# Transposes by way of DRAM in a hybrid RWKV-7 / HGRN-2 layer on one core: blocks of turned tiles stored and loaded a row at a time, and fourteen head ends turned on VectorE instead of TensorE

## The chip, the core and the metric

The kernel runs on one NeuronCore of a Trainium2 chip, as one launch. Its engines run side by side, each through its own list of instructions in order: TensorE (PE, matmuls into PSUM), VectorE (DVE), ScalarE (ACT), GpSimd (POOL) and SyncE (SP), which issues nearly all DMAs. An instruction that waits holds up whatever stands behind it on its engine. The metric is the device time of one execution in microseconds (us); lower is better.

## The reference, cut to what matters

One layer over 512 frames of 2048 channels. A combined input projection feeds 16 RWKV heads of 64 channels and 8 HGRN heads of 128; their gated outputs go through one output projection, a residual and a LayerNorm. With the scans left to their names:

```python
proj = einsum('btd,dc->btc', h, w_in)
rw = token_shift(proj[..., :RWKV_COLS], shift_mu)
hg = proj[..., RWKV_COLS:]
# RWKV, per head of 64
o = rwkv7_scan(r, decay, k, v, -kk, kk * a)
o = (o - mean(o)) * rsqrt(var(o) + GN_EPS) * gn_w + gn_b
o = o + sum(r * k * r_k) * v
o_rwkv = o * silu(z)
# HGRN, per head of 128, in chunks of 64 frames
o = hgrn2_chunkwise(q, log_f, k, i)
o_hgrn = o * rsqrt(mean(o * o) + RMS_EPS) * g_norm_w * silu(z)
y = concat([o_rwkv, o_hgrn]) @ w_out
h = layer_norm(ALPHA * h + y, ln_w, ln_b)
```

All of it is float32; setup_inputs draws x, the weights and the gains.

## The kernel before, in words

**Stages.** Activations lie with channels on the 128 partitions and 512 frames along the free dimension. The input projection is a sequence of units; a unit is one block of 128 output channels, 16 steps over the input channels, and each step takes three products of 128x128 by 128x512 (`three`, L453 before; high and low parts of both operands, so that the sum has float32 accuracy). These go to PSUM banks with the tag `main`, and are called projection products below. Weights stream from `w_all` in pieces `wr` of 512 KB, two pieces buffered; ACT makes the high part `wh` of each half and DVE the low part `wl` (three buffers each). The output projection comes last: four column blocks of 512, the first of them (`d = 0`) over 16 gated channel blocks in the order 0 to 5, 8 to 13, 14, 6, 15, 7. These sixteen steps of the first block are called steps 0 to 15; step 11 takes block 13, step 12 block 14, step 13 block 6 and step 15 block 7. A gated block k is a tile `g`, split into `xh` (ACT) and `xl` (DVE) just before its step. Twelve of the gated blocks are put into the DRAM tensor `spill` and loaded back; 6, 7, 14 and 15 stay on chip. During step 8 the 2 MB of LayerNorm weights are loaded, broadcast to all partitions (`big<-ln_wb`).

**Mixers.** Beside the projections, and put in between their products, run the mixers. RWKV goes by pairs of heads (8 pairs, p = 0 to 7), two pairs to a group: `rwkv_prep`, then `rwkv_invert` and `rwkv_scan` for the group, then `outputs`, then `rwkv_finish` for each pair (group norm, bonus, gate). HGRN goes by head (h = 0 to 7), two at a time, ending in `hgrn_out`.

**What sets the order.** The order on each engine is written out when the program is built, by a planner (`Plan`): generators yield operations, and the planner puts an operation into its engine's list when, by its own cost table, the operands will be there. For a DMA the planner books a fixed time. Nothing is reordered on the chip.

**Turning.** Several tiles have to be transposed, from frames on the partitions to channels on the partitions or back:
- In `rwkv_prep`, `bk` (128 x 8 x 128) and `v` (128 x 512, into the lower half of `zz`) go through `turned`: one DVE transpose (`dtr`, L366), which turns each 32x32 block within itself, and then small DMAs, one for each 32x32-block position, that carry the blocks to their places from SBUF to SBUF (L401): 16 DMAs of 32 KB for each `bk`, 8 of 32 KB for each `v`.
- In `rwkv_finish` the normed output `o_all` is turned on TensorE: four transposes (`tr`, L328) into a PSUM bank `mix`, which DVE then reads in `stt`.
- In `hgrn_out` the same is done with four transposes of `o2`. Three further transposes for each head turn `k` earlier in that function.

Of the kernel before, what the change touches and what calls it, by code (L numbers as in the profile page):

```python
# [15 lines left out]
P = 128  # L16
# [225 lines left out]
def mixer_kernel(ctx, tc, head, x_r, w_all, par, up, ln_wb, consts, hmask, out):  # L242
# [148 lines left out]

    def turned(dst, src, tmp, rows=4, base=0):


        name = dst.tensor.name
        yield dtr(tmp, src)
        yield lambda: by_now(tmp)
        for a in range(4):
            for b in range(rows):
                o = base + 32 * b  # L400
                nc.sync.dma_start(dst[o : o + 32, :, 32 * a : 32 * a + 32],  # L401
                                  tmp[32 * a : 32 * a + 32, :, 32 * b : 32 * b + 32])
# [218 lines left out]

    hc = [slice(64 * h, 64 * h + 64) for h in range(2)]

    def rwkv_prep(S, p):
# [114 lines left out]
        yield room(zz=1)  # L739
        z = take("zz", [P, NCH, P])  # L740
        yield room(ksq=1)
        tmp = take("ksq")
        yield from turned(z, chunks(v), chunks(tmp), rows=2, base=64)
        drop(v, tmp)
        S["zz"] = z

    def from_v(SS, sc):

        yield lambda: all("zz" in S for S in SS)
        zs = [S["zz"] for S in SS]  # L750
        yield room(main=2, mix=1)
        yield landed(*zs, sc)
        pss = [take("main") for _ in SS]
        for half, (z, ps) in enumerate(zip(zs, pss)):
            for c in range(NCH):
                for h in range(2):
                    yield mm(ps[hc[h], c * C : c * C + C], sc[64:128, 0, half * 16 + 2 * c + h],
                             z[64:128, c, hc[h]])

        def keep():  # L760
            for z, ps in zip(zs, pss):
                for h in range(2):
                    yield copy(z[0:64, :, hc[h]], chunks(ps[hc[h]]))
                drop(ps)

        return keep

    def outputs(SS, sc):
# [3 lines left out]
        for half, (S, po) in enumerate(zip(SS, pss)):  # L772
            z = S["zz"]
            yield lambda z=z: by_now(z)
            for c in range(0, NCH, 2):
                for h in range(2):
                    for e in range(2):
                        yield mm(po[hc[e], c // 2 * P + 64 * h : c // 2 * P + 64 * h + 64],
                                 sc[:, 1, half * 16 + 2 * (c + e) + h], z[:, c + e, hc[h]])
        for S, po in zip(SS, pss):  # L780
# [51 lines left out]
    def rwkv_scan(SS, sc):  # L832
# [9 lines left out]
        def block(ps, h):  # L842
            return ps[hc[h], h * 64 : h * 64 + 64]

        for rt, bds, o in zip(rts, bdss, os):
            yield memset(rt[64:128], 0.0)
# [4 lines left out]
        for c in range(NCH):  # L851
            more = c < NCH - 1
            zs = [zz[:, c] for zz in zzs]
            news = [bds[c % 2] for bds in bdss]
            pxs = []
            if c > 0:
# [5 lines left out]
                for rt, px, z in zip(rts, pxs, zs):  # L862
                    yield stt(rt[0:64], px[0:64, :P], -1.0, z[0:64], ALU.mult, ALU.subtract)
                if more:
                    for new, old, pc in zip(news, olds, pcs):
                        yield act(new, old, AF.Copy, scale=pc[:, c : c + 1])
            else:
                for rt, z in zip(rts, zs):
                    yield copy(rt[0:64], z[0:64], scale=-1.0)
            yield landed(*rts)  # L870
# [5 lines left out]
            for psa, z in zip(psas, zs):  # L876
                for h in range(2):
                    yield copy(z[0:64, hc[h]], block(psa, h))
                drop(psa)
# [17 lines left out]
    def rwkv_finish(S, p):  # L897
# [31 lines left out]

    def rwkv_group(SS, grp):  # L930
# [4 lines left out]
        def run():  # L935
# [3 lines left out]
            for i, S in enumerate(SS):  # L939
                plan.add(finishes, rwkv_finish(S, 2 * grp + i))  # L940

# [115 lines left out]
    def hgrn_out(S, h, q, k, dt_, dg, tot, tots):  # L1057
# [37 lines left out]
        S["used"]()  # L1095
        yield landed(o2)
        pn = take("mix")
        for j in range(4):
            yield tr(pn[:, j * P : j * P + P], o2[:, j * P : j * P + P])
        yield has(S, "g")  # L1100
        yield stt(g, pn, hcol(HHW, h), S["g"], ALU.mult, ALU.mult)
        drop(S["g"], pn, o2)
        put_gated(8 + h, g)
# [28 lines left out]
    scans = [plan.queue(), plan.queue()]  # L1132
    groups, finishes, preps = plan.queue(), plan.queue(), plan.queue()
    heads, stores = plan.queue(), plan.queue()
# [532 lines left out]
```

## Time and profile before

| what | value |
|---|---|
| runs | median 1050.85 us of 3 (1050.78 to 1051.72) |
| the profiled execution's own time | 1050.24 us |
| its span, first to last instruction | 1048.5 us |
| granted TensorE clock | 0.999 |
| DMA packets, MB | 87305, 114.79 |
| packets under 512 bytes | 56368 |
| transposes on TensorE (L328) | 88 |
| DMAs at L401 | 192 of 32 KB |

Busy shares are averages over stages with different limits. In the lists of groups, the number behind the bar is the group's busy time and its mean duration in ns; durations of matmuls overlap, since their ends are modelled, so the distance between the starts of two matmuls is what one costs. "Idle before" is the time the engine stood before those instructions and what ended it.

### The profile page before, as it was taken

The page shows a single profiled execution, that of the slowest core. Times are in us where ns is not written, and L with a number is a line of the kernel's source. Part 1 is how long each engine was busy: PE and PEld are TensorE (multiplying, and loading weights), DVE is VectorE, ACT ScalarE, POOL GpSimd, SP SyncE. Part 2 cuts the span into 40 slices and gives each one's busy share as a digit, 9 for nine tenths or more (in the row PEclk, how much of TensorE's full clock was granted, in tenths as well). Part 3 has the DMA queues.
Part 4 walks back from the last instruction along what each step waited for, and adds up shares of the span by engine and source line. Part 5 has one row for each costly group of instructions (what it writes and reads, how often), then busy time and mean ns, then how long its engine had stood idle before and what let it go on. Part 6 is the DMA issues. An engine that isn't in the chain of part 4 may idle for free.

```text
span 1048.5 us, 18840 instructions
## 1 busy us (share of the span) xinstructions
PE 1040.6 (99%) x7342; PEld 865.1 (83%) x7342; DVE 755.7 (72%) x1653; ACT 437.6 (42%) x867; POOL 38.3 (4%) x81
## 2 busy tenths in 40 slices
PE   9999999999999999999999999999999999999997
PEld 8888888888888888888888888888888888888885
DVE  7465898667759987676689866865998778625556
ACT  6545333445353354452533353525334554323321
POOL 0000000000000000000000000000000002000000
PEclk9999999999999999999999999999999999999999
DMA  8134342222343522223534323234352244545613
GB/s 332 54 103 114 99 109 86 86 79 81 84 123 100 122 82 74 78 98 79 138 78 118 98 62 96 70 96 110 100 128 72 69 164 131 182 131 159 202 60 131
DMA packets 87305, 114.79 MB, mean 109 GB/s; under 512 B 56368, under 2 KB 58160, under 8 KB 87088
## 3 DMA queue, kind: packets, MB, share of 16 engines
q1 hardware_dynamic: 87072, 113.39, 36.6%
q8 instruction: 58, 0.95, 0.4%
q14 instruction: 31, 0.25, 0.1%
q10 hardware_dynamic: 144, 0.20, 0.1%
HBM read 99.92 MB, written 7.34 MB: 102 GB/s over the span
## 4 chain that ended last, share of the span: by engine, by line
PE 99%; DVE 1%; DVEq 0%; issue 0%
PE main L453 74%; PE mix L324 11%; PE mix L453 8%; PE main L1192 3%; PE main L324 2%; PE mix L328 1%; PE mix L1142 0%; DVE inv L356 0%; DVE inv L347 0%; DVE stats L1549 0%; DVEq L1663 0%; DVE mv L1357 0%; DVE bd L356 0%; DVE mv L352 0%; DVE inv L1140 0%
## 5 line engine op out<-in xcount | busy, mean ns | idle before, releaser
L453 PE MATMUL main<-xl,wh 128*128 128x512 f32 x864 | 341.1, 395 | 0.0
L453 PE MATMUL main<-xh,wl 128*128 128x512 f32 x864 | 341.1, 395 | 0.0
L453 PE MATMUL main<-xh,wh 128*128 128x512 f32 x864 | 340.9, 395 | 0.0
L337 ACT ACTIVATE wh<-wr 128x512 fp32r<-128x512 f32 x299 | 186.9, 627 | 237.1 <-PE main L453 180.5
L347 DVE TENSOR_TENSOR wl<-wr,wh 128x512 fp32r<-128x512 f32 x299 | 203.8, 682 | 61.8 <-ACT wh L337 60.1
L453 PEld LDWEIGHTS main<-xh,wh 128*128 128x128 f32 x864 | 162.4, 188 | 33.0
L453 PEld LDWEIGHTS main<-xh,wl 128*128 128x128 f32 x864 | 162.5, 188 | 32.6
L453 PEld LDWEIGHTS main<-xl,wh 128*128 128x128 f32 x864 | 162.4, 188 | 32.6
L453 PE MATMUL main<-wl,xh 128*128 128x512 f32 (+1 forms) x262 | 102.6, 392 | 0.0
L453 PE MATMUL main<-wh,xh 128*128 128x512 f32 (+1 forms) x262 | 102.1, 390 | 0.0
L453 PE MATMUL main<-wh,xl 128*128 128x512 f32 (+1 forms) x262 | 101.6, 388 | 0.0
L453 PEld LDWEIGHTS main<-wh,xh 128*128 128x128 f32 x262 | 49.2, 188 | 9.9
L453 PEld LDWEIGHTS main<-wh,xl 128*128 128x128 f32 x262 | 49.2, 188 | 9.7
L453 PEld LDWEIGHTS main<-wl,xh 128*128 128x128 f32 x262 | 49.2, 188 | 9.6
L338 ACT ACTIVATE t<-main,om 128x512 f32<-128x512 f32 x33 | 22.4, 687 | 51.1 <-PE main L453 41.6
L356 DVE SCALAR_TENSOR_TENSOR t<-main,pr,t 128x511 f32<-128x511 f32 x33 | 24.4, 747 | 26.5 <-ACT t L338 26.2
L347 DVE TENSOR_TENSOR inv<-inv,inv 64x30 f32<-64x30 f32 (+14 forms) x120 | 38.6, 322 | 2.9
L347 DVE TENSOR_TENSOR inv<-inv 64x30 f32<-64x30 f32 (+14 forms) x120 | 38.4, 320 | 2.3
L347 DVE TENSOR_TENSOR t<-t,tot 128x256 f32<-128x256 f32 x96 | 37.8, 414 | 1.8 <-PE mix L324 1.7
L356 DVE SCALAR_TENSOR_TENSOR bd<-mix,pc,bd 64x64 f32<-64x64 f32 x112 | 31.7, 283 | 7.5 <-PE mix L324 5.2
L337 ACT ACTIVATE zz<-mix 64x64 f32<-64x64 f32 x63 | 13.8, 220 | 46.9 <-PE mix L324 45.8
L338 ACT ACTIVATE t<-main 128x512 f32<-128x512 f32 x32 | 18.5, 598 | 30.7 <-PE main L453 30.2
(222 smaller groups left out, 1328.0 us busy)
## 6 DMA issues: line engine op xcount, KB each, us to landing
wr<-w_all SPq DMA_DIRECT2D x156, 512.0 KB, 3.6
q<-head SPq DMA_DIRECT2D x15, 448.0 KB, 5.9
q<-q SPq DMA_DIRECT2D x128, 32.0 KB, 2.4
g<-x_r SPq DMA_DIRECT2D x16, 256.0 KB, 3.8
spill<-g SPq DMA_DIRECT2D x12, 256.0 KB, 2.7
out<-q SPq DMA_DIRECT2D x12, 256.0 KB, 2.4
t<-spill SPq DMA_DIRECT2D x10, 256.0 KB, 4.2
zz<-ksq SPq DMA_DIRECT2D x64, 32.0 KB, 2.6
```

Of the source, the lines that this page charges most:

```text
L324: return Op([("pe", cost, lambda: pe.matmul(o, l, r, start=start, stop=stop, **kw))], [l, r], [o], mode="narrow" if narrow else "main" if ...
L328: return Op([("pe", 0.11, lambda: pe.transpose(o, i, ident))], [i], [o])
L337: return "act", cost, lambda: sc_e.activation(o, i, f, scale=scale)
L338: return "act", cost, lambda: sc_e.activation(o, i, f, scale=scale, bias=bias)
L347: return dve_op([a, b], o, lambda: dve.tensor_tensor(o, a, b, f), base=0.16 if o.shape[0] < P and size(o) == C and o.tensor.name in tags e ...
L356: return dve_op([a, b], o, lambda: dve.scalar_tensor_tensor(o, a, s, b, f1, f2), per=0.00113, base=0.085 if o.shape[0] == P else 0.25 if s ...
L453: pe.matmul(ps, l, r, start=first and i == 0, stop=last and i == 2)
L1192: pe.matmul(pss[a], *ops, start=k == 0 and low == of == 0, stop=k == KT - 1 and low == 1)
```

## The change

`turned` no longer places blocks from SBUF to SBUF. After the DVE transpose, whose result is now laid out by rows of blocks, one DMA stores the whole tile to a new DRAM tile `far` (512 KB for `bk`, 256 KB for the others), the generator waits until the planner's clock is 3.0 us on, and then one DMA for each row of blocks loads it into place: 4 loads of 128 KB for `bk`, 2 of 128 KB for `v`, 4 of 64 KB for the others. The planner books the data as there 4.5 us after the loads.

The result of `turned` for `bk` lands in the old `bk` tile in another layout, so a copy of 128 x 1024 brings it into `tmp`, which becomes `bk`. `zz` keeps the layout by blocks, and the code that reads it is changed to match.

The ends are turned in the same way: all eight `rwkv_finish`, and `hgrn_out` for heads 0 to 5 (heads 6 and 7 keep their TensorE transposes). In place of DVE's `stt` from PSUM, an ACT operation now applies the gain (and for RWKV the bias) while it reorders the blocks, and DVE multiplies from SBUF. The two pairs of a group now finish on two queues of the planner instead of one.

In all, the program has 5641 matmul instructions instead of 5697 (56 transposes fewer), 50 DVE transposes instead of 36, 863 ACT operations instead of 846, and 376 DMAs on SP instead of 434. Counted over the order, PE goes from projection products into products on part of the array (small tiles) 33 times instead of 30.

```diff
+    def turned(dst, src, tmp, base=0):
+        c = src.shape[1]
+        n = src.shape[2] // 32
+        yield dtr(tmp, src.rearrange("p c (b f) -> p b c f", f=32))
         yield lambda: by_now(tmp)
-        for a in range(4):
-            for b in range(rows):
-                o = base + 32 * b
-                nc.sync.dma_start(dst[o : o + 32, :, 32 * a : 32 * a + 32],
-                                  tmp[32 * a : 32 * a + 32, :, 32 * b : 32 * b + 32])
-            at = plan.clock["pe"] + 0.4 * rows
-            yield lambda: plan.clock["pe"] >= at
-        plan.ready[name] = (plan.clock["pe"] + 3.0, "dma")
+        far = dpool.tile([4, 32, n, c * 32], F32, tag=nm("far"), name=nm("far"))
+        nc.sync.dma_start(far.rearrange("a p b r -> (a p) b r"), tmp.rearrange("p b c f -> p b (c f)"))
+        plan.busy[tmp.tensor.name] = (plan.clock["pe"] + 3.0, "dma")
+        at = plan.clock["pe"] + 3.0
+        yield lambda: plan.clock["pe"] >= at
+        for b in range(n):
+            o = base + 32 * b
+            nc.sync.dma_start(dst[o : o + 32].rearrange("p a c f -> p a (c f)"),
+                              far[:, :, b].rearrange("a p r -> p a r"))
+        plan.ready[dst.tensor.name] = plan.busy[dst.tensor.name] = (plan.clock["pe"] + 4.5, "dma")
...
@@ rwkv_prep
-        yield from turned(bk, bk, tmp)
-        drop(tmp)
+        flat = bk.rearrange("p c t -> p (c t)")
+        yield from turned(blocks(flat, NCH), bk, blocks(tmp.rearrange("p c t -> p (c t)"), NCH))
+        yield copy(tmp.rearrange("p c (a f) -> p a c f", f=32), blocks(flat, NCH))
+        drop(bk)
+        S["bk"] = tmp
...
@@ rwkv_finish
-        drop(sm, sq)
+        drop(sm)
+        yield from turned(blocks(S["ot"], 4), o_all, blocks(sq.rearrange("p a b -> p (a b)"), 4))
+        drop(sq)
...
         sz = take("ksq")
...
-        yield landed(o_all)
-        po = take("mix")
-        for j in range(4):
-            yield tr(po[:, j * P : j * P + P], o_all[:, j])
         yield act(sz, z, AF.Tanh, scale=0.5)
-        yield stt(g, po, hcol(HGW, p), S["bv"], ALU.mult, ALU.add)
-        drop(po)
+        yield act(in_blocks(g), blocks(S["ot"], 4).rearrange("p a c f -> p c a f"), AF.Identity,
+                  scale=hcol(HGW, p), bias=hcol(HGB, p))
         yield stt(z, sz, 1.0, z, ALU.add, ALU.mult)
-        yield stt(g, g, hcol(HGB, p), z, ALU.add, ALU.mult)
+        yield tt(g, g, S["bv"], ALU.add)
+        yield tt(g, g, z)
...
@@ hgrn_out
+        if h < 6:
+            yield room(ksq=1)
+            tmp = take("ksq")
+            yield from turned(blocks(o2, 4), tiles(o2), blocks(tmp, 4))
+            drop(tmp)
+            yield has(S, "g")
+            yield act(in_blocks(g), blocks(o2, 4).rearrange("p a c f -> p c a f"), AF.Copy, scale=hcol(HHW, h))
+            yield tt(g, g, S["g"])
+            drop(S["g"], o2)
```

How the order moves is shown at three places, all in the first block of the output projection, where the last pairs (6 and 7) and the last HGRN head (7) finish.

TensorE, step 11 of that block, before: `main_8896` and `main_8938` are PSUM banks of the output, `xh_9338` and `xl_9339` the parts of gated block 13, `t_7607` the normed output of RWKV pair 7.

```order
L453 MATMUL main_8896<-wh_9318,xh_9338 128x512
L328 MATMUL mix_9368<-cst,t_7607 128x128 x4
L453 MATMUL main_8896<-wl_9319,xh_9338 128x512
L453 MATMUL main_8896<-wh_9318,xl_9339 128x512
L453 MATMUL main_8938<-wh_9318,xh_9338 128x512
```

The same step in the changed program; `xh_9270` is gated block 13 there, and `t_7899` the normed output of HGRN head 7.

```order
L464 MATMUL main_8861<-wh_9248,xh_9270 128x512
L464 MATMUL main_8861<-wl_9249,xh_9270 128x512
L328 MATMUL mix_9301<-cst,t_7899 128x128 x4
L464 MATMUL main_8861<-wh_9248,xl_9271 128x512
L464 MATMUL main_8869<-wh_9248,xh_9270 128x512
```

The transposes of pairs 6 and 7 are gone from PE's list; those of head 7 are the only ones left in the output projection, and stand at step 11.

ScalarE around the same step, before, with the counters that each instruction waits for: `xh_9338` is the split of block 13 (step 11), `ksq_9349` the tanh of pair 7's gate, `xh_9361` and `xh_9394` the splits for steps 12 and 13.

```order
L337 ACTIVATE xh_9307<-t_9179 128x512 [waits DMAHW4_49]
L337 ACTIVATE wh_9318<-wr_9199 128x512 [waits PE_49,Activation_49]
L337 ACTIVATE xh_9338<-t_9209 128x512 [waits DMAHW6_49]
L337 ACTIVATE wh_9351<-wr_9273 128x512 [waits DMAHW7_49,PE_49,Activation_49]
L337 ACTIVATE xh_9361<-g_9000 128x512
L338 ACTIVATE ksq_9349<-t_8898 128x512
L337 ACTIVATE wh_9382<-wr_9273 128x512 [waits DVE_49,PE_49]
L337 ACTIVATE xh_9394<-g_9227 128x512
```

And now, from the split for step 10 (`xh_9238`) on: `ksq_9265` is the tanh of pair 6's gate, `g_9264` the new operation that applies pair 6's gain to the loaded blocks.

```order
L337 ACTIVATE xh_9238<-t_9130 128x512 [waits DMAHW0_49]
L337 ACTIVATE wh_9248<-wr_9152 128x512 [waits PE_49,Activation_49]
L338 ACTIVATE ksq_9265<-t_8751 128x512 [waits DMAHW5_49,DVE_49]
L337 ACTIVATE xh_9270<-t_9158 128x512 [waits DMAHW2_49]
L337 ACTIVATE wh_9281<-wr_9202 128x512 [waits DMAHW3_49,PE_49,Activation_49]
L337 ACTIVATE xh_9293<-g_8890 128x512
L338 ACTIVATE g_9264<-t_6988,half 128x512 [waits DMAHW2_49,DMAHW7_49,DMAHW1_49,DMAHW0_49]
L337 ACTIVATE wh_9314<-wr_9202 128x512 [waits DVE_49,PE_49]
L338 ACTIVATE ksq_9328<-t_8863 128x512 [waits DVE_49,Activation_49]
```

The tanh of pair 6 now stands ahead of the split for step 11, and waits for a landing: its tile `ksq` is one of two, and the one it takes held pair 6's turned blocks, which the store to `far` reads. The value that it waits for on DMAHW5 is the one that this store sets when it has landed.

SyncE's DMAs at the LayerNorm weights, before:

```order
L430 DMA wr_9273<-w_all 128x1024 [waits DMAHW2_49,DVE_49]
L1473 DMA big_9283<-ln_wb 128x4096 [waits DMAHW0_49,PE_49]
L430 DMA wr_9323<-w_all 128x1024 [waits DMAHW5_49,DMAHW1_49,DVE_49]
L1456 DMA g_9365<-x_r 128x512
L430 DMA wr_9389<-w_all 128x1024 [waits DMAHW7_49,DMAHW3_49,DVE_49]
```

And in the changed program (`far_9229` belongs to pair 6, `far_9288` to pair 7; the loads into `t_6988` are pair 6's four):

```order
L441 DMA wr_9202<-w_all 128x1024 [waits DMAHW6_49,DVE_49]
L1500 DMA big_9214<-ln_wb 128x4096 [waits DMAHW4_49,PE_49]
L401 DMA far_9229<-ksq_9122 128x512 [waits DMAHW5_49,DVE_49]
L441 DMA wr_9253<-w_all 128x1024 [waits DMAHW1_49,DVE_49]
L407 DMA t_6988<-far_9229 32x4x128 [waits DMAHW7_49,DMAHW5_49]
L407 DMA t_6988<-far_9229 32x4x128 [waits DMAHW0_49]
L407 DMA t_6988<-far_9229 32x4x128
L407 DMA t_6988<-far_9229 32x4x128 [waits DMAHW2_49]
L401 DMA far_9288<-ksq_9124 128x512 [waits DMAHW3_49,DVE_49]
L1483 DMA g_9297<-x_r 128x512 [waits DMAHW4_49]
L441 DMA wr_9321<-w_all 128x1024 [waits DVE_49]
L407 DMA t_7605<-far_9288 32x4x128 [waits DMAHW6_49,DMAHW3_49]
```

Pair 6's store now stands directly behind the 2 MB load of LayerNorm weights, and its four loads, which wait for that store, stand ahead of pair 7's store.

More of the change, by code (lines that the diff above doesn't have):

```diff
@@ L622, in mixer_kernel @@
     hc = [slice(64 * h, 64 * h + 64) for h in range(2)]
+    hb = [slice(2 * h, 2 * h + 2) for h in range(2)]
     def rwkv_prep(S, p):
@@ L739, in rwkv_prep @@
         yield room(zz=1)
-        z = take("zz", [P, NCH, P])
+        z = take("zz", [P, 4, NCH, 32])
         yield room(ksq=1)
         tmp = take("ksq")
-        yield from turned(z, chunks(v), chunks(tmp), rows=2, base=64)
+        yield from turned(z, chunks(v), blocks(tmp, NCH), base=64)
         drop(v, tmp)
@@ L852, in rwkv_scan @@
             more = c < NCH - 1
-            zs = [zz[:, c] for zz in zzs]
+            zs = [zz[:, :, c] for zz in zzs]
             news = [bds[c % 2] for bds in bdss]
@@ L877, in rwkv_scan @@
                 for h in range(2):
-                    yield copy(z[0:64, hc[h]], block(psa, h))
+                    yield copy(z[0:64, hb[h]], by32(block(psa, h)))
                 drop(psa)
@@ L939, in run @@
             for i, S in enumerate(SS):
-                plan.add(finishes, rwkv_finish(S, 2 * grp + i))
+                plan.add(finishes[i], rwkv_finish(S, 2 * grp + i))
         plan.add(scans[0], run())
@@ L1095, in hgrn_out @@
         S["used"]()
[L1096 to L1102, printed above, removed]
+        if h < 6:
[7 more added lines that the diff above has]
+            drop(S["g"], o2)
+        else:
+            yield landed(o2)
+            pn = take("mix")
+            for j in range(4):
+                yield tr(pn[:, j * P : j * P + P], o2[:, j * P : j * P + P])
+            yield has(S, "g")
+            yield stt(g, pn, hcol(HHW, h), S["g"], ALU.mult, ALU.mult)
+            drop(S["g"], pn, o2)
         put_gated(8 + h, g)
@@ L1132, in mixer_kernel @@
     scans = [plan.queue(), plan.queue()]
-    groups, finishes, preps = plan.queue(), plan.queue(), plan.queue()
+    groups, finishes, preps = plan.queue(), [plan.queue(), plan.queue()], plan.queue()
     heads, stores = plan.queue(), plan.queue()
```

19 lines of the change are left out of this document (11 added, 8 removed).

## The prediction, made before the changed kernel ran

> **What bounds the kernel now.** First the page: the busy shares, then the chain that ended last by engine.
>
> ```profile
> PE 1040.6 (99%) x7342; PEld 865.1 (83%) x7342; DVE 755.7 (72%) x1653; ACT 437.6 (42%) x867; POOL 38.3 (4%) x81
> PE 99%; DVE 1%; DVEq 0%; issue 0%
> L453 PE MATMUL main<-xl,wh 128*128 128x512 f32 x864 | 341.1, 395 | 0.0
> ```
>
> PE is busy for 1040.6 of the 1048.5 us of the span, the chain lies on it for 99%, and the largest group of projection products has 0.0 us of idle time before it. So the time is the sum of what PE's instructions cost one after the other: work taken off PE shortens the run, work added elsewhere is free, until something makes PE wait. A busy PE is no proof of speed, so I take costs from distances between starts. The chain in order of time has one block of 192 projection products without anything between (start, length, what):
>
> ```profile
> 907.23 43.52 PE mix L453 x192
> ```
>
> 43.52 / 192 = 0.227 us for one.
>
> **What leaves PE.** Fourteen groups of four transposes. PE's timeline around one of them (start, length, instruction):
>
> ```profile
> 892.98 0.39 PE L453 MATMUL main<-wh,xh 128*128 128x512 f32 x1
> 893.21 0.60 PE L328 MATMUL mix<-cst,t 128*128 128x128 f32 x4
> 893.56 0.48 PE L453 MATMUL main<-wl,xh 128*128 128x512 f32 x1
> 893.88 0.40 PE L453 MATMUL main<-wh,xl 128*128 128x512 f32 x1
> ```
>
> From the start of the product before to the second product behind there are 0.90 us; two products alone take 0.454. One group costs 0.45 us, fourteen 6.3 us. Against it stand three more changes into small tiles, in PE's timeline so:
>
> ```profile
> 186.13 0.39 PE L453 MATMUL main<-xh,wh 128*128 128x512 f32 x1
> 186.44 0.70 PE L324 MATMUL mix<-t 128*32 128x32 f32 x32
> ...
> 188.37 0.50 PE L453 MATMUL main<-xl,wh 128*128 128x512 f32 x1
> 188.71 0.39 PE L453 MATMUL main<-xh,wl 128*128 128x512 f32 x1
> ```
>
> On entering, 0.31 us pass instead of 0.23; on leaving, 0.34 instead of 0.23: 0.19 us a change, 0.6 for three. **PE's own list gets 5.7 us shorter** (5.2 if some groups shared their change of mode, 6.3 if the small tiles cost nothing).
>
> **What the other engines get.** The turning on DVE, and the DMAs it used, have these rows (the last is the time from issue to landing of the DMAs at L401):
>
> ```profile
> L366 DVE STREAM_TRANSPOSE ksq<-t x8: 698/700/706, 83.4 to 771.4; 128x512 f32<-128x512 f32 x8
> L401 SPq DMA_DIRECT2D q<-q x128: 585/608/1292, 74.9 to 768.5; - x128
> ...
> DMA to landing us min/median/max: 1.9/2.5/4.8
> ```
>
> Fourteen more DVE transposes are 9.8 us, with 8 copies of 128x1024 (about twice a 128x512 operation, 0.6 us by the rows below, so 1.2 each, on ACT or DVE) 19 us at most. DVE then stands at 775 of some 1045 us: hidden under PE. ACT gets 14 operations of 0.6 us, 9 us, at 42%. The 16 small DMAs of a `bk` held SP for 16 x 0.61 = 9.7 us and now 5 DMAs do: SP gains. All this costs nothing by itself. What can cost is where an instruction waits for one of the new landings with something behind it that PE needs.
>
> **The last pairs: where the new wait bites.** DMAs by size, median from issue to landing:
>
> ```profile
> wr<-w_all SPq DMA_DIRECT2D x156, 512.0 KB, 3.6
> q<-q SPq DMA_DIRECT2D x128, 32.0 KB, 2.4
> g<-x_r SPq DMA_DIRECT2D x16, 256.0 KB, 3.8
> spill<-g SPq DMA_DIRECT2D x12, 256.0 KB, 2.7
> big<-ln_wb SPq DMA_DIRECT2D x1, 2048.0 KB, 10.1
> ```
>
> In quiet times a 256 KB store takes 2.7 us. But the order puts pair 6's store right behind `ln_wb`. What happens to a DMA there is to be seen before the change: first SP's timeline (start, length, issue):
>
> ```profile
> 884.70 0.33 SPq L430 DMA_DIRECT2D wr<-w_all  x1
> 885.13 1.26 SPq L1473 DMA_DIRECT2D big<-ln_wb  x1
> 890.09 0.33 SPq L430 DMA_DIRECT2D wr<-w_all  x1
> 890.47 0.50 SPq L1456 DMA_DIRECT2D g<-x_r  x1
> ```
>
> Then the landing of that last row's DMA alone:
>
> ```profile
> DMA to landing us min/median/max: 6.6/6.6/6.6
> ```
>
> And the stretch as a window, with the busy share of the DMA engines and their GB/s at the end of the row:
>
> ```profile
> 890.00:895.00 5.00, 5.00 (x25) 4.14 (x24) 4.39 (x9) 2.83 (x5) 1.64 (x1) 1.00 0.96 377
> ```
>
> `ln_wb`, issued at 885.13, landed 10.1 us later, at 895.2. The 256 KB of `x_r`, issued 5.3 us behind it, landed at 897.1, after 6.6 us instead of 3.8: it waited for `ln_wb` to drain. So pair 6's store lands between 10.1 and 11.9 us after the issue of `ln_wb`; there is no 512 KB between, so I take 10.7. [...]
>
> Now the clock from a zero: PE's last product of `outputs` for pairs 6 and 7. The durations come from these rows of DVE, ACT and POOL:
>
> ```profile
> 876.31 0.68 DVE L347 TENSOR_TENSOR wl<-wr,wh 128x512 fp32r<-128x512 f32 x1
> 876.91 0.17 DVE L353 TENSOR_SCALAR sm<-sm 128x8 f32<-128x8 f32 x1
> 883.99 0.69 DVE L347 TENSOR_TENSOR wl<-wr,wh 128x512 fp32r<-128x512 f32 x1
> 875.49 0.62 ACT L337 ACTIVATE wh<-wr 128x512 fp32r<-128x512 f32 x1
> 876.01 0.62 ACT L337 ACTIVATE xh<-t 128x512 fp32r<-128x512 f32 x1
> 877.15 1.64 POOL L379 TENSOR_TENSOR sm<-sm,mhalf 128x8 f32<-128x8 f32 x1 [9.47 <-DVE sm L353]
> ```
>
> From start to start, as in the timelines of these engines, a wide DVE operation takes 0.60, a wide ACT operation 0.52. (1) In DVE's list, 15 wide operations lead from zero to the `wl` that frees the buffer for the next `wr`: 9.0 us. POOL's square root (1.64) is done by then. Before, `wr` went out 0.1 us after that `wl` (883.99 + 0.6, then 884.70) and `ln_wb` 0.43 after it; so `ln_wb` goes out at 9.5. Pair 6's turned blocks are ready at 9.7, SP is busy with `ln_wb` for 1.26: the store goes out at 10.8. (2) It lands at 9.5 + 10.7 = 20.2. (3) ACT's tanh of pair 6 waits for that landing, and the split for step 11 stands behind it: 20.2 + 2 x 0.52 = 21.3. (4) PE has 75 projection products from zero to the first that needs this split: 17.1. **PE waits 4.2 us.** Before, the same tanh waited for no DMA. (5) Then DVE has to make the low part and to scale head 7's output, 1.2 us, ahead of the four transposes that follow two products later: 0.8 more. (6) Pair 6's four loads follow the store at 0.61 us each, the last at 22.0, and land 2.5 later, at 24.5. Gain, gate, split: three ACT and three DVE operations and their handing over, about 3.5 us, 28.0; by then PE has got to step 13 only (21.3 + 0.8 + 26 products = 28.0). No wait. (7) Pair 7's store goes out behind those loads at 22.6 and lands at 25.3; ahead of its loads a `wr` waits for DVE (26.6); loads from 27.0 to 28.8, behind 512 KB in the queue, land at about 31.3; three operations each on ACT and DVE make it 34.4 for step 15, which PE reaches at 33.5: 0.9. **Sum for the tail 5.9 us**: 4.3 with the store at the early bound and no wait for pair 7, 7.7 with it at the late bound.
>
> **The other ends.** At the end of the first group the order has a 512 KB store, its four loads, a weight load, the two ends' stores and eight loads one behind the other on SP. The planner books 3.0 us for a store; by the rows above, one queued behind four loads and a `wr` takes about 4, and the loads (3 x 0.6 + 2.5 = 4.3) add nothing. The operation of ACT that waits for them has the next pair's squares behind it, whose products PE takes up without anything between: 0 to 2 us, taken as 1.0. In the second group the two ends are apart from `bk`, in the third the weight splits behind the wait have about 3 us of lead: nothing. The six HGRN ends store 256 KB in a quiet queue (2.7, booked 3.0): nothing, 0.5 each if a landing is late.
>
> **Sum.** -5.7 + 5.9 + 1.0 = +1.2 us. The profiled execution took 1050.24 us, 0.6 less than the median of the runs shown (1050.85), so 1051.4 for an execution like it and 1052.0 beside the median. No stage ends earlier behind the tail, so nothing of this is absorbed.
>
> **The rivals.** A difference under 0.2%, 2.1 us, is about what a measurement of this kernel cannot tell from none.
>
> *Forecast:* the saving is spent in the tail, 1052.0; alone it reaches from 1048.9 (-6.3 + 4.3) to 1055.3 (-5.2 + 7.7 + 2.0). Chance 0.48.
>
> *No wait in the tail:* the store is not held by `ln_wb`, since the DMA engines interleave its packets with those of `ln_wb` instead of taking them behind. Then it takes the 2.7 of a quiet time, lands at 13.5, the split for step 11 is there at 14.6, before 17.1, and only the saving and the 1.0 stay: 1046.1. For it: PE never waited in 1050 us under this planner. Against: the `x_r` row. Chance 0.12.
>
> *A shorter queue:* the DMA engines keep 377 GB/s, as in the window row, from the start: 2.3 MB in 6.2 us and 1.9 ahead of the first bytes (an estimate from the shortest landing of a small DMA) make 8.1, the store lands at 17.6, step 11 waits 1.6, its transposes 0.8: 1050.85 - 5.7 + 2.4 + 0.9 = 1048.5. Chance 0.14.
>
> *Slower:* every new end makes an in-order engine wait, not just the last. ACT's gain operation stands in its list among the copies of the scan, whose chain PE follows closely. If landings are 1 us later than booked at each of the six HGRN ends (0.5 each) and 2 us are lost at each of three group ends, with the late bound in the tail: 1050.85 - 5.7 + 7.7 + 3 + 6 = 1061.9; with half of the middle waits 1057.4. It is slower from 2.1 us of waits beyond the saving, so from 7.8 us in all. For it: SP issues stores, loads and weights in one list, and in the first group four transfers follow each other. Against: with three `wh` buffers, of 12 products each, the weight splits can be up to 24 x 0.227 = 5.4 us ahead of PE. [...] Chance 0.26.
>
> **The numbers.** Faster by over 0.2% (below 1048.75): 0.12, half of the shorter queue, and 0.04 of the forecast, 0.23. Slower (above 1052.95): 0.26 and 0.12 of the forecast, 0.38. The same: 0.39. Range 1047.0 to 1057.5: it leaves out the case without a wait and the upper part of the slow one.
>
> **What would show it.** Right: L328 has 32 transposes; PE's idle time, none before, shows 4 to 6 us near the first output block, ended by ACT's `xh`, and ACT waiting there for the DMA `far`; the landing of that store 9 us and more. Wrong: pair 6's store landing within 4 us; PE without idle time there; idle time of PE spread over the scans.

## The result and the profile after

The changed kernel took 1064.49 us in the median of four runs (1064.44 to 1065.72), the kernel before 1050.82: a ratio of 1.0132, interval 1.0114 to 1.0149. It is 13.7 us slower. The forecast was 1052.0 with a range of 1047.0 to 1057.5, so the time lies outside the range, on the side to which the forecast leaned.

The page of the changed kernel, busy time of PE and the shares of the chain that ended last, which stood at 99% PE before:

```profile
PE 1041.5 (98%) x7286; PEld 859.8 (81%) x7286; DVE 763.4 (72%) x1672; ACT 449.6 (42%) x884; POOL 38.0 (4%) x81
PE 83%; DMA 8%; DVE 4%; ACT 2%; issue 1%; SPq 1%; POOL 0%; ACTq 0%; DVEq 0%
```

The span grew from 1048.5 to 1062.7 us, but PE's busy time by 0.9 only, and the chain now runs over DMA, DVE and ACT too. PE waits. For whom, says the view of the waits (in total, times, longest, us), first in the kernel before, then in the changed one, where the rows of 1.5 and 1.1 us are there still:

```profile
PE mix L324 <- ACT ksq L1409: 1.5, 1, 1.5
PE mix L1142 <- DVE inv L1140: 1.1, 1, 1.1
PE mix L324 <- DVE bd L356: 0.4, 1, 0.4
```

```profile
PE main L464 <- ACT xh L337: 4.6, 2, 3.2
PE mix L324 <- DVE ksq L347: 3.2, 5, 1.6
PE mix L324 <- ACT ksq L337: 2.4, 3, 1.1
PE mix L324 <- ACT ksq L1436: 1.5, 1, 1.5
PE mix L324 <- ACT zz L337: 1.2, 1, 1.2
PE mix L1169 <- DVE inv L1167: 1.1, 1, 1.1
PE main L464 <- ACT wh L337: 1.0, 2, 0.6
PE mix L328 <- DVE t L347: 0.7, 1, 0.7
```

These are gaps behind the modelled end of a product, which lies 0.16 us behind the start of the next in quiet running (0.39 long, 0.23 apart). The whole loss is seen from start to start: for every two neighbours on PE, their distance less the usual distance of such a pair in the kernel before. Excesses of over 0.25 us sum to 17.4 us, against 0.5 before: 6.0 in the first output block, 5.8 ahead of the products with `ones_r` at 86, 135, 557 and 774 us, 3.5 at the end of the first group (290 to 297), 1.4 at 682, 0.7 in two small ones.

**The tail.** ACT's timeline there, then PE's (in brackets the idle time before and what ended it):

```profile
893.39 0.63 ACT L337 ACTIVATE wh<-wr 128x512 fp32r<-128x512 f32 x1 [1.58 <-PE main L464]
900.69 0.63 ACT L338 ACTIVATE ksq<-t 128x512 f32<-128x512 f32 x1 [6.66 <-DMA far<-ksq]
901.22 0.61 ACT L337 ACTIVATE xh<-t 128x512 fp32r<-128x512 f32 x1
```

```profile
901.89 0.50 PE L464 MATMUL main<-wh,xh 128*128 128x512 f32 x1 [3.15 <-ACT xh L337]
902.23 0.40 PE L464 MATMUL main<-wl,xh 128*128 128x512 f32 x1
903.31 1.09 PE L328 MATMUL mix<-cst,t 128*128 128x128 f32 x4 [0.69 <-DVE t L347]
```

The landing of the one store that the tanh waits for, issued at 891.56:

```profile
DMA to landing us min/median/max: 9.0/9.0/9.0
```

The tanh in the `ksq` buffer waits for the store, the split for step 11 stands behind it, and PE behind that, as the prediction had it. But something follows that it did not have. Windows before, during and after the wait (the third number from the end is the granted TensorE clock):

```profile
890.00:898.00 8.00, 8.00 (x37) 6.63 (x36) 5.86 (x11) 2.21 (x4) 3.05 (x2) 1.00 0.82 291
898.00:902.60 4.60, 1.45 (x6) 0.57 (x4) 0.73 (x2) 1.91 (x4) 0.00 (x0) 1.00 0.69 264
902.70:906.10 3.40, 2.79 (x9) 2.44 (x10) 3.32 (x6) 1.74 (x4) 0.00 (x0) 0.50 0.69 188
906.10:912.00 5.90, 5.90 (x28) 4.85 (x27) 3.99 (x7) 2.09 (x4) 0.00 (x0) 1.00 0.67 165
```

Right behind the wait the clock is at a half for 3.4 us, in which PE is busy for 2.79. Wide products in it start 0.43 us apart instead of 0.23, so about half of these 2.79, an estimated 1.4 us, are lost as well.

**The middle.** The group of ACT's new copies of `bk`, all six that ACT has (DVE makes the other two), with its idle time before them:

```profile
L337 ACT ACTIVATE q<-q 128x1024 f32<-128x1024 f32 x6 | 6.4, 1062 | 23.4 <-DMA q<-far 23.4
```

ACT stands for 23.4 us ahead of six copies, 3.9 each. What that does at the second one, on ACT and then on PE:

```profile
132.73 1.06 ACT L337 ACTIVATE q<-q 128x1024 f32<-128x1024 f32 x1 [6.50 <-DMA q<-far]
133.70 0.61 ACT L337 ACTIVATE wh<-wr 128x512 fp32r<-128x512 f32 x1
134.22 0.61 ACT L337 ACTIVATE ksq<-t 128x512 fp32r<-128x512 f32 x1
```

```profile
134.88 0.50 PE L324 MATMUL mix<-ksq,ones_r 128*128 128x512 f32 x1 [0.94 <-ACT ksq L337]
136.25 0.50 PE L324 MATMUL mix<-ksq,ones_r 128*128 128x512 f32 x1 [0.86 <-DVE ksq L347]
```

The high part of `r` (`ksq<-t`) stands behind the copy in ACT's list, and PE has reached its product with `ones_r`. Why the copy waits is on SP, here at the first `bk`:

```profile
74.39 0.33 SPq L441 DMA_DIRECT2D wr<-w_all  x1
74.77 0.43 SPq L401 DMA_DIRECT2D far<-q  x1
79.97 1.75 SPq L407 DMA_DIRECT2D q<-far  x4
```

The store goes out 0.4 us behind a weight load of 512 KB, and the loads wait for it. Its landing:

```profile
DMA to landing us min/median/max: 5.1/5.1/5.1
```

At the second `bk`, whose copy is the one shown above, the store had no weights close ahead, but the loads had:

```profile
121.10 0.33 SPq L401 DMA_DIRECT2D far<-q  x1
124.17 0.33 SPq L441 DMA_DIRECT2D wr<-w_all  x1
124.61 2.57 SPq L407 DMA_DIRECT2D q<-far  x4
```

The landing of this store, and then that of its four loads:

```profile
DMA to landing us min/median/max: 2.6/2.6/2.6
```

```profile
DMA to landing us min/median/max: 5.9/6.5/6.7
```

The planner books 3.0 us for a store and 4.5 for a set of loads: at the first `bk` the store was late, at the second the loads. The loads of the first, with no weights close ahead, took 2.5 to 2.9. Of the 30 stores, 19 landed later than booked: in quiet times one takes 2.0 (256 KB) or 2.6 us (512 KB), behind a `wr` 4.4 and 5.1, behind `ln_wb` 9.0.

### The profile page after: what moved, and what is told of

Same layout as the page of the kernel before. It is cut to its first block, busy times and chain, and to the rows that moved or that the text cites. A ratio compares the mean times of both kernels' runs of the same rounds, so it can differ in the third digit from the quotient of the medians.

```text
span 1062.7 us, 18731 instructions
## 1 busy us (share of the span) xinstructions
PE 1041.5 (98%) x7286; PEld 859.8 (81%) x7286; DVE 763.4 (72%) x1672; ACT 449.6 (42%) x884; POOL 38.0 (4%) x81
## 4 chain that ended last, share of the span: by engine, by line
PE 83%; DMA 8%; DVE 4%; ACT 2%; issue 1%; SPq 1%; POOL 0%; ACTq 0%; DVEq 0%
PE main L464 59%; PE mix L324 10%; PE mix L464 8%; PE main L1219 3%; DMA wr<-w_all 2%; DMA far<-ksq 2%; PE main L324 2%; DMA t<-far 2%; DMA q<-far 1%; DVE wl L347 1%; SPq L407 1%; DVE t L347 1%; DMA far<-q 0%; ACT wh L337 0%; DVE inv L356 0%
## 5 line engine op out<-in xcount | busy, mean ns | idle before, releaser
L464 PEld LDWEIGHTS main<-wh,xl 128*128 128x128 f32 x262 | 49.5, 189 | 10.2 <-DVE xl L347 0.4
L338 ACT ACTIVATE ksq<-t 128x512 f32<-128x512 f32 (+1 forms) x24 | 15.1, 630 | 43.7 <-DVE t L347 21.6
```

Source lines behind the costliest of these rows:

```text
L338: return "act", cost, lambda: sc_e.activation(o, i, f, scale=scale, bias=bias)
L464: pe.matmul(ps, l, r, start=first and i == 0, stop=last and i == 2)
```

## The experiments

Each ran beside the kernel before on the same chip. Theory A was formed from the profile above: waits come from landings later than booked, at in-order engines that have PE's work behind the waiting instruction; 6.0 us of them in the tail, 11.4 in the middle.

**1. The last two pairs on TensorE.** In `rwkv_finish`:

```
+        if p < 6:
...
+        else:
+            yield landed(o_all)
+            po = take("mix")
+            for j in range(4):
+                yield tr(po[:, j * P : j * P + P], o_all[:, j])
...
```

> Only the ends of RWKV pairs 6 and 7 go back to TensorE; everything else stays as in the changed kernel. Theory A (PE's waits add up: 6.0 us at steps 11 to 15 of the first output block, some 11 us in the middle): the 6.0 us go, two groups of four transposes come back (0.9), 1064.5 - 6.0 + 0.9 = 1059.4, and the waits in the middle stay where they are. Rival B (the last stage has little slack anyway, and ACT waits for something else there): 1063 or more.

Measured 1059.44 us, ratio 1.0083 (1.0070 to 1.0097). As theory A says, to the microsecond, but partly by luck: the stretch of half clock at the end went as well (1.4 us, not in the sum; mean clock 1.000), and 1.8 us of small new waits came elsewhere. The tail cost what it was said to cost, and rival B falls.

**2. Only `bk` back within SBUF**, by the 16 DMAs of the old `turned`, here called `placed`.

```
...
-        yield from turned(blocks(flat, NCH), bk, ...)
-        yield copy(tmp.rearrange(...), blocks(flat, NCH))
...
+        yield from placed(bk, bk, tmp)
...
```

> Only bk goes back to the sixteen small DMAs within SBUF, without the copy behind them; v and all ends stay by way of DRAM. Theory A (the copy of bk stands in ACT's list and waits for a landing that comes later than it was booked, with squares behind it that PE needs): the waits of PE ahead of the ones_r products at about 86, 135, 557 and 774 us go (1.0 + 2.2 + 1.7 + 0.8 = 5.7 us), and a part of the 3.5 us at 290: 1057 to 1059. Rival B (the ends crowd ACT and SP in the middle, bk is innocent): 1063 to 1065.

Measured 1074.82 us, ratio 1.0226 (1.0212 to 1.0240): neither theory, and 10 us slower than the changed kernel. The waits at 86, 135, 557 and 774 us went, as theory A says, but others of 3.0 to 4.0 us came, at 476, 511, 735 and in the tail, and half clock for 30.7 us in all (mean clock 0.985). SP's timeline before the one at 511, and ACT's:

```profile
500.02 4.79 SPq L420 DMA_DIRECT2D q<-q  x7
504.92 0.54 SPq L456 DMA_DIRECT2D wr<-w_all  x1
505.56 0.38 SPq L401 DMA_DIRECT2D far<-ksq  x1
```

```profile
509.52 0.63 ACT L337 ACTIVATE wh<-wr 128x512 fp32r<-128x512 f32 x1 [2.53 <-DMA wr<-w_all]
```

The small DMAs hold SP, 0.6 us each, and weights and stores queue behind them; here the weight load comes late and PE waits 4.0 us. Beside the stores and loads for the ends, the old placing crowds SP as it did not in the kernel before. The wait of 3.4 us at 476 is another matter: there PE waits for DVE to read a bank, with no small DMA near, and its cause stays open. So this run does not show what the copy of `bk` cost by itself.

**3. The other half alone: all ends on TensorE.**

```
-        if h < 6:
+        if h < 0:
```

and in `rwkv_finish` the old end for all pairs.

> The other half alone: bk and v by way of DRAM, all fourteen ends back on TensorE. PE's own list is then 0.5 us longer than before the change. Theory A (bk's landings cost about 6 to 7 us by themselves): 1050.8 + 0.5 + 6 to 7 = 1057 to 1058.5, slower than the kernel before. Rival B (bk is free, as the prediction had it): 1051.3.

Measured 1058.91 us, ratio 1.0086 (1.0073 to 1.0100). That is 0.4 us above theory A's range, and rival B falls: `bk` and `v` by way of DRAM cost 8 us by themselves and save nothing on PE. The prediction had booked this part at nothing. ACT waited 29.8 us ahead of the eight copies, and of PE's 8.0 us of excess 7.3 stand ahead of products with `ones_r`.

**4. Bookings that count what SP has issued.**

```
+    def behind(n):
+        plan.clock["dma"] = max(plan.clock["dma"], plan.clock["pe"]) + 4 * n * 128 / 360e3
+        return plan.clock["dma"] + 2.0
...
-        at = plan.clock["pe"] + 3.0
+        at = behind(size(tmp))
...
-        plan.ready[...] = (plan.clock["pe"] + 4.5, "dma")
+        plan.ready[...] = (behind(c * n * 32) + 0.4 * n + 0.9, "dma")
```

> Same transfers, same transposes; only the planner's booking changes: a store or a load to or from far is put behind the bytes that SP has already issued (weights, LayerNorm weights), instead of a fixed 3.0 and 4.5 us. Theory A (landings later than booked, so that engines wait with work behind): with later bookings the waiting instructions move behind the work that was held up, most of the 11 us in the middle go, and most of the 6 us at the end: 1046 to 1049, faster than the kernel before. Rival C (what comes later makes the mixers late, the wait only moves to another place): 1058 or more.

Measured 1062.24 us, ratio 1.0110 (1.0097 to 1.0124). The time lies in rival C's range, and theory A is half right: in the middle PE's excess fell from 11.4 to 2.6 us (1.5 more came at 880, just ahead of the tail), and ACT's idle time ahead of `bk`'s copies by almost a half, though now all eight are ACT's:

```profile
L337 ACT ACTIVATE q<-q 128x1024 f32<-128x1024 f32 x8 | 8.4, 1056 | 13.0 <-DMA q<-far 13.0
```

The tail got worse. PE's largest wait, and the instruction of ACT in front of it:

```profile
PE main L468 <- ACT xh L337: 8.3, 1, 8.3
```

```profile
900.03 1.27 ACT L338 ACTIVATE ksq<-t 128x512 f32<-128x512 f32 x2 [6.62 <-DMA far<-ksq]
```

The stores of the two pairs go out at 895.5 and 896.9 there, behind a `wr`, and 10.2 us of half clock come with the wait (mean clock 0.993). Theory A had been too hopeful: these bookings give pairs 6 and 7 no time that the order of the steps does not have. That no other booking would is argued, not shown.

**5. Both: later bookings, and the last two pairs on TensorE.** The edits of 1 and 4.

> The later bookings of the run before, and the ends of pairs 6 and 7 on TensorE. PE's list is 4.7 us shorter than before the change. Theory A (waits come from landings later than booked; in the last block no booking can help, since the steps of blocks 6 and 7 follow too soon): the three small waits of that run at 180, 250 and 300 us stay (2.6 us), nothing else does, the clock stays full: 1050.6 - 4.7 + 2.6 = 1048.5, 1047.5 to 1050. Rival C (what the bookings push back returns as a wait elsewhere): 1053 or more.

Measured 1052.83 us, ratio 1.0018 (1.0009 to 1.0027), between the two theories. The tail's waits are gone. Ahead of it, 6.3 us of excess are left, the largest 1.7 at 186 us, with a stretch of half clock behind it (wide products 0.43 us apart from 186.2 to 189.6), and 1.6 at 305 to 307. Its runs go from 1049.73, with the clock at 1.000 in the mean, to 1054.25.

**6. LayerNorm weights late.**

```
-            if j == 8:
+            if j == 14:
```

> The changed kernel, but the 2 MB of LayerNorm weights are issued at step 14 of the first output block instead of step 8. Theory A (pair 6's store waits for these 2 MB): the store lands in 2 to 4.5 us instead of 9.0; the 6.0 us of waits at steps 11 to 15 fall to about 1, and the stretch of half clock that follows the wait at step 11 (3.4 us, 1.7 us lost) goes too: 1064.5 - 6.0 - 1.7 + 1.0 = 1057.8. Rival D (the weights or the bandwidth hold the store, not the 2 MB): it lands after 7 us or more, 1063 or more.

Measured 1063.78 us, ratio 1.0130 (1.0116 to 1.0143). The store landed in 4.0 us, behind a `wr`, instead of 9.0: rival D falls. PE's excess in the tail went from 6.0 to 2.6 us, but a stretch of half clock stayed there, another followed the waits at 135 us (mean clock 0.996, 0.998 in the changed kernel), and waits at 8 and 686 us cost 1.6 us more than in the changed kernel. So the mechanism is right and the time did not follow it.

**7. The transfers on another queue**, stores and loads alike.

```
-        nc.sync.dma_start(far...)
+        nc.gpsimd.dma_start(far...)
```

> The changed kernel with all stores to and loads from far issued by GpSimd, on its own queue, instead of SyncE; same bytes, same places in the program, same bookings. Theory E (SP's queue is taken in order, so a store behind a weight load of 512 KB lands 2.5 us later, in 4.4 or 5.1 us instead of 2.0 or 2.6): on another queue nearly all stores land in 2 to 3 us, the waits in the middle fall from 11 to 4 us or less and the one at the end by half: 1050 to 1054. Rival F (the sixteen DMA engines are shared, whatever the queue): the stores behind weights land in over 4 us still, 1061 to 1066.

Measured 1082.70 us, ratio 1.0307 (1.0292 to 1.0321), worse than both theories. From the DMA issues:

```profile
far<-ksq POOLq DMA_DIRECT2D x22, 256.0 KB, 3.1
far<-q POOLq DMA_DIRECT2D x8, 512.0 KB, 5.1
q<-far POOLq DMA_DIRECT2D x32, 128.0 KB, 3.8
```

The stores of 256 KB land in 3.1 us in the median instead of 3.9, those of 512 KB in 5.1 instead of 4.8, and loads of `bk` in 3.8 instead of 3.2. So in this run a queue of its own did not free `bk` of the weights, and GpSimd held each issue for 0.55 us in a list in which the loads wait for the stores. ACT waits 30.4 us for `bk`, and PE's waits reach 3.6 us, with 20.5 us of half clock (mean clock 0.989). What the queue alone does to a landing stays open, since the run also moves the issues into GpSimd's list.

**8. The clock by itself.** In the kernel before, where weights are split:

```
+    MORE = {60: 6, 90: 8, 120: 10, 150: 12, 180: 14, 210: 16, 240: 18}
...
+                for _ in range(MORE.get(i, 0)):
+                    sc_e.activation(parts[i][0], raws[...], AF.Copy)
                 yield from split(*parts[i], raws[...])
```

> The kernel before, with the high part of seven pieces of weights computed 6, 8, 10, 12, 14, 16 and 18 times too often on ScalarE before it is right (0.52 us each, unseen by the planner), so that PE waits at seven places for growing times. Theory G (a wait of PE of some 3 us brings its clock to a half for 3.4 us or a multiple, and each such stretch costs another 1.7 us): the short waits leave the clock alone, the long ones are followed by a stretch at 0.5, and the run is longer than the sum of the waits by 1.7 us for each. Rival H (the clock falls for another reason): granted clock 1.0 throughout, and the run is longer by the waits alone.

Measured 1097.98 us, ratio 1.0449 (1.0435 to 1.0464): 47.6 us longer. The stretches at half clock as windows (behind the length: PE's busy time; third from the end: the clock):

```profile
183.60:193.70 10.10, 9.68 (x156) 7.88 (x153) 6.00 (x17) 5.41 (x12) 0.00 (x0) 0.50 0.19 54
508.00:514.50 6.50, 5.96 (x16) 4.55 (x17) 3.75 (x7) 2.04 (x4) 2.02 (x1) 0.50 0.38 100
603.50:610.00 6.50, 3.72 (x110) 2.54 (x114) 3.67 (x12) 3.64 (x7) 0.00 (x0) 0.50 0.00 0
719.50:726.00 6.50, 3.25 (x10) 2.77 (x11) 2.37 (x7) 3.52 (x8) 0.00 (x0) 0.50 0.00 0
822.00:828.50 6.50, 3.23 (x8) 2.51 (x9) 3.11 (x7) 4.62 (x8) 0.00 (x0) 0.50 0.00 0
```

PE's waits sum to 35 us in its view, 32 more than before. PE was busy for 25.8 us of the windows above, of which a half, an estimated 12.9, is lost: 45 of the 47.6. Rival H falls. The price of a stretch was not theory G's 1.7 us each time, but half of PE's busy time in it, 1.6 to 4.8. The four longest waits, of 3.8 us and over, each have a stretch behind them. But so has one of 1.7 us at 183, where PE was on small tiles, while two of 1.8 and 2.1 us near 300 have none.

**9. The copy of `bk` after `v`.** With the fixed bookings:

```
-        yield copy(tmp.rearrange(...), blocks(flat, NCH))
...
         yield from turned(z, chunks(v), blocks(tmp, NCH), base=64)
         drop(v, tmp)
+        yield copy(flipped.rearrange(...), blocks(flat, NCH))
...
```

> The changed kernel with its old fixed bookings, but the copy of bk that follows its loads is issued only after v has been turned too, some 15 us later, so that the loads have landed when ACT or DVE come to it. Theory A (the copy waits in ACT's list for the loads, and the squares behind it hold up PE's products with ones_r): ACT's 23.4 us of waiting for these loads go, PE's waits at 86, 135, 557 and 774 us (5.8 us) go; those at the ends (290, 681 and the last block) stay: 1058 to 1060. Rival B (what PE waits for there is the store and load traffic as such): 1063 or more.

Measured 1057.72 us, ratio 1.0078 (1.0065 to 1.0092). The same traffic, and ACT's 23.4 us are 3.6, for all eight copies:

```profile
L337 ACT ACTIVATE q<-q 128x1024 f32<-128x1024 f32 x8 | 8.4, 1046 | 3.6 <-DMA q<-far 3.6
```

The time is just below theory A's range, but in part by luck. What it says of the copy holds: the four waits of 5.8 us ahead of the products with `ones_r` are gone with the same traffic, so there it was the place of the waiting instruction that cost, and rival B falls. Elsewhere the order moved. New excesses of 5.9 us came, among them 2.3 at 501 to 504 and 1.7 at 722 us, where ACT stands before an end's gain operation, with the high part of `r` behind it:

```profile
499.81 0.81 ACT L338 ACTIVATE g<-t,half 128x512 f32<-128x512 f32 x1 [6.10 <-DMA t<-far]
```

In return the tail lost 2.7 instead of 6.0 us, the end of the first group 2.3 instead of 3.5, and the wait at 682 is gone. So 5.8 us is what the copy's place cost; the time saved is the sum of all of these.

**10 to 12. Put together.** All three have the edits of 1 and 4. The tenth adds the late copy; the eleventh adds 1.0 us to each store's booking and 1.1 to each set of loads; the twelfth adds the late copy, 0.5 and 0.6 us (lines of run 4 against those of the twelfth):

```
-        at = behind(size(tmp))
+        at = behind(size(tmp)) + 0.5
...
-        plan.ready[...] = (behind(c * n * 32) + 0.4 * n + 0.9, "dma")
+        plan.ready[...] = (behind(c * n * 32) + 0.4 * n + 1.5, "dma")
```

> The late copy, the bookings behind what SP has issued, and pairs 6 and 7 on TensorE, all together. PE's list is 4.7 us shorter than before the change. Theory A: the wait at 300 us (1.3) falls with the copy, some 2 to 3 us of small waits stay, and with no wait near 3 us the clock stays full: 1050.4 - 4.7 + 2.5 = 1048, at most 1050 with one stretch of half clock. Rival C (each saving on PE is eaten by a wait elsewhere): 1052 or more.

> As the run with later bookings and pairs 6 and 7 on TensorE, but with 1.0 us more booked for each store and 1.1 us more for each set of loads. PE's list is 5.2 us shorter than before the change. Theory A (what was left of ACT's waits for far, 13.5 us for bk and 5 for the ends, is still bookings that are too short): ACT's waits for far fall to under 8 us, PE's waits to about 3: 1048, 1047 to 1050. Rival C: 1052 or more.

> The late copy together with 0.5 us more for each store and 0.6 us more for each set of loads, pairs 6 and 7 on TensorE. PE's list is 4.9 us shorter than before the change. Theory A: ACT hardly waits for far any more (under 5 us in all), PE's waits are 2 us: 1047.5, 1046.5 to 1049.5. Rival C: 1052 or more.

Measured 1049.52 us (ratio 0.9992, 0.9983 to 1.0001), 1049.42 (0.9985, 0.9976 to 0.9993) and 1047.52 (0.9972, 0.9961 to 0.9984). The last beats both kernels, by 3.1 us against the one before. All of PE's waits in it, of which the second and third stand in the kernel before too:

```profile
PE mix L324 <- issue: 1.6, 1, 1.6
PE mix L324 <- ACT ksq L1457: 1.5, 1, 1.5
PE mix L1190 <- DVE inv L1188: 1.1, 1, 1.1
```

The list of PE is 4.9 us shorter and 3.1 are kept. The wait of 1.6 us stands in the midst of 64 equal small products at 602 us, with 6.8 us of half clock behind it in this execution (mean clock 0.997). It ends on "issue": the profile shows nothing that PE waits for, so it is no late landing, and its cause is open. Other runs of the kernel, with the clock at 1.000 in the mean, took 1046.7 and 1046.8.

## Why the prediction was wrong, point by point

*What bounds the kernel, and what leaves PE:* right. PE has no slack, every wait is paid in full, and without waits the shorter list shows: the twelfth run has the new transposes for 12 of the 14 ends and is faster.

*The last pairs:* right in mechanism, and in the sum of the waits. Worked out were 4.2 us at step 11, 0.8 at head 7's transposes, nothing before step 13 and 0.9 at step 15, 5.9 in all; measured were 3.3, 0.8, 0.35 and 1.6, 6.0 (the 0.35 has no wait in the view and lies in the stretch of half clock). `ln_wb` landed in 8.8 us instead of 10.1 and the store 9.0 behind its own issue, 9.5 behind that of `ln_wb`, where 10.7 was taken. The measured 9.5 lies below both of the bounds taken from the rows before (10.1 and 11.9). The late bound was also summed wrongly: 1.2 us on the 5.9 give 7.1 for the tail, not 7.7.

*"The other ends", taken as 1.0 us:* this is the step that failed. It measured 11.4. Two things were wrong in it. The first was to count ends only. The waits that cost most there, 5.8 us, have nothing to do with an end: they come from the copy of `bk`, which the prediction costed as 1.2 us of hidden ACT work, in the paragraph that ended "All this costs nothing by itself". The sentence behind it named the right test, an instruction that waits for a new landing with something behind it that PE needs; it was not put to ACT's list in `rwkv_prep`. There the copy stands ahead of the split of `r`. Runs 3 and 9 show it: `bk` and `v` alone cost 8 us, and with the copy moved away these waits of 5.8 us go.

The second was to take the landing of a store from the quiet rows, 2.7 us against 3.0 booked. The 2.7 was the median of twelve stores for which no engine waited, and it is no quiet row: in the trace of the kernel before, six of these `spill` stores landed in 2.0 to 2.2 us and the six others in 3.2 to 6.1. What decided here is the 512 KB in front, 2.4 to 2.5 us more for a store, and for the loads of the second `bk` 5.9 to 6.7 us against 4.5 booked. The prediction used such a sign for `ln_wb` alone: `x_r` behind the 2 MB took 6.6 us instead of 3.8.

*The price of a wait:* the prediction summed waits at their own length. The granted clock was 0.999 before, so no row of that trace had the other price: behind some waits PE runs at half clock for 3.4 us or a multiple, with some 1.4 us lost in the changed kernel and 12.9 in run 8.

*The rivals:* no wait in the tail did not happen. A shorter queue, which had the store land 8.1 us behind the issue of `ln_wb`, was about as far off as the forecast's 10.7 (9.5 measured), but its wait of 1.6 us at step 11 was half of the real one. "Slower" gave 1057.4 to 1061.9 and came nearest, with its mechanism, every new in-order wait; but it put the price on the HGRN ends and the group ends. Of its three group ends only the first cost more than 0.3 us (3.5), of the six HGRN ends one (1.4 at 682). Of the prediction's signs, all of the right ones came, and one of the wrong ones as well: idle time of PE spread over the scans. Transposes left on TensorE were the faster ones against the changed kernel (1050.8 us with all of them there, 1064.5 with fourteen groups off it) and at the last two pairs (1059.4 with these back on it); but the twelfth run has twelve groups of four off TensorE and takes 1047.5, 1050.6 with all on it.

*The sum as measured:* -5.7 from the list, +17.4 of waits less the 0.5 of before, +1.4 of half clock make 12.6 of the 14.2 us by which the span grew. The -5.7 is the forecast's figure. Counted from the trace, PE's distances without the excesses and without the stretch of half clock are only 3.7 us shorter than before, and there the last 1.6 lie: small waits of under 0.25 us, or a smaller saving. In the twelfth run the same count gives 5.0, by its list 4.9.

## What to carry to other kernels

Where one in-order engine bounds the kernel, as PE does here, a new transfer costs less by its bytes than by the instruction that waits for it, and by what is queued behind that instruction on its engine: the twelfth run keeps most of the new traffic and is faster than the kernel before. So go through every engine's list for each new wait, the harmless copies first, and put the waiting instruction where the landing is long past: here that took away the waits of 5.8 us behind one harmless copy. Take the landing of a DMA with what its queue holds in front of it (a store behind 512 KB landed 2.4 to 2.5 us later here), not from a quiet row, and leave on the bound engine what is needed within a few microseconds, as the last two pairs were here.

## What the runs showed of the hardware

A wait of PE has a second price. In the trace of the changed kernel the clock is at 0.50 behind the wait in the tail for 3.41 us (902.66 to 906.08); but for the time behind the last product, it records no other half clock. In run 8 it is at 0.50 throughout windows of 6.50 and 10.10 us. The 6.8, 10.2, 20.5 and 30.7 us of half clock in runs 12, 4, 7 and 2 are 2, 3, 6 and 9 times 3.41.

The length of a wait does not decide alone. Stops of 1.5 to 1.7 us among small tiles were enough at 183 us of run 8 and at 186 us of run 5, while waits of 1.8 and 2.1 us near 300 us of run 8 had no half clock behind them. The stretches at full clock between two changes, 897.71 and 157.01 us in the changed kernel and 1041.07 in the kernel before, are 263, 46 and 305 times 3.413, so in these two traces the changes fall on a grid. In the changed kernel the step of that grid just ahead of the half clock (899.25 to 902.66) has PE busy for 0.73 us. The next lowest up to 1035 us (295.09 to 298.50) has 1.77, and the clock stays full behind it. The waits at 135 us fall into two steps there (131.25 to 134.66 to 138.08), in which PE is busy for 2.69 and 2.33, with no half clock behind either. So a wait near 2 us seems to count by where it falls, an estimate from these few steps. What exactly counts as idle, among small tiles above all, is open.

This may be one reason why runs of one kernel differ: the twelfth ranges from 1045.98 to 1049.04 us, with a mean clock of 0.997 or 0.998 in the three longer executions and of 0.999 or 1.000 in the three shorter; the kernel before ranges from 1050.01 to 1051.01 beside it. It is not the only one: in the tenth, three executions at 1.000 took 1049.49 to 1050.71, the shortest, 1048.08, had 0.999.

In the changed kernel a store to DRAM of 256 KB landed in 2.0 us on a quiet queue and in 4.4 right behind a 512 KB load on it, one of 512 KB in 2.6 and 5.1: a load in front cost a store 2.4 to 2.5 us. The four loads of a `bk` landed in 2.5 to 2.9 us at 80 us, and in 5.9 to 6.7 at 125, 0.4 us behind a 512 KB load.
